# Attention's logits in a two-layer encoder trunk: the second product over 64 rows becomes one over 128

## The chip, the cores and the metric

The kernel runs on one core of one Trainium2 chip. The time is device microseconds of one execution; a profile records one execution and is a run of its own. The core has five engines with a queue of instructions each: TensorE (PE in the rows; its weight loads are shown apart as PEld), VectorE (DVE), ScalarE (ACT), GpSimd (POOL) and SyncE (SP). Each engine takes its own instructions in order and waits for the others by semaphores. Transfers between memory and the core's buffers are issued by SP, ACT or POOL.

## What is computed

Two layers over 512 frames of 1024 channels. In each layer a projection feeds a sparse attention with 8 heads of 64 channels, whose keys are chosen by an indexer, and a gated linear attention with 4 heads; both are merged, normalised, and followed by a gated convolution and feed-forward part. What matters here, from the reference:

```python
score = jnp.einsum('bqhs,bqh->bqs', jax.nn.relu(dots), wb.astype(F32) * (IDX_HEADS ** -0.5))
top_val, top_idx = lax.top_k(score, topk)
...
logits = jnp.einsum('bqhd,bqkhd->bhqk', qb.astype(F32), k_sel.astype(F32)) * (Dh ** -0.5)
logits = jnp.where(valid[:, None], logits, -jnp.inf)
p = jax.nn.softmax(logits, axis=-1)
return jnp.einsum('bhqk,bqkhd->bqhd', p, v_sel.astype(F32)).astype(q.dtype)
```

## The kernel before

Nearly all products work on float32 numbers split in two: a high part in the narrower format that TensorE takes, and the low part that is left (`split`, L145 on ScalarE for the high part and L146 on VectorE for the low one). A product of two split numbers is three products (`mm3`, L151 to L153). Weights come in tiles of 512 KB by SP, three raw tiles in flight and five split ones, and are split when a place is free.

The projections of queries and keys come out with one channel of each head per partition and are copied to device memory by GpSimd's queue, split (`staged`, L498), as a tile that holds the 64 high parts of a head in its first 64 rows and the 64 low parts in the others. `load_task` reads them back for two heads at a time: the keys as they are (L525), so that partitions 0 to 63 hold the high part of a head and 64 to 127 its low part, and the queries' high part into both halves of a tile (L529, two reads) with the low part in the first half of another (L530).

So a product of the queries' tile with the keys' tile over all 128 rows gives high times high plus high times low at once (L668), and a second one over 64 rows adds low times high (L669). `softmax_steps` does this for one head: four blocks of 128 queries, `qb` 0 to 3, against 128, 256, 384 and 512 keys. Both products go into one of two banks (`sps`), VectorE adds the mask and takes the maximum (L672), ScalarE takes the exponential (L675), VectorE divides (L676, L677). `values_steps` transposes (L697) and multiplies with the values (L706 to L709). The indexer's scores (L547 and L548) have two products over 128 rows each.

Attention is a task of generators that move on by two steps whenever the main work, a projection, has done a few products (`tick`). The order on each engine is settled when the program is built: the instructions are ordered by priorities and by modelled times, weight splits and the copies of projections out of their banks ahead of the rest. A change of the code can therefore move instructions that it doesn't touch.

Around the change the main work is, in this order: the queries' projection, the keys' (`ak`), the values' (`av`), and eight tiles of a gate (`gr_tile`), into which attention is woven. The four accumulation banks of `ak` are copied out and used again by `av`. At the same time the linear attention ends: VectorE takes the variance (L332), GpSimd its power -0.5 (L333), VectorE refines it (L336 to L339) and makes a shift (L646), ScalarE applies both (L652).

Of the kernel before, what the change touches and what calls it, by code (L numbers as in the profile page):

```python
# [10 lines left out]
F32 = mybir.dt.float32  # L11
# [45 lines left out]
class Trunk:  # L57
# [457 lines left out]
    def load_task(self, dr, dst, low=None):  # L515

        rows = dr.rearrange("(q h) n -> q h n", h=HEADS)
        load = self.nc.gpsimd.dma_start
        for _ in range(4):
            yield  # L520
        for hp in range(4):
            src = rows[:, 2 * hp:2 * hp + 2]
            t = self.u()
            if low is None:
                load(t.bitcast(F32), src)  # L525
            else:
                lo = self.u()
                for j in range(2):
                    load(t[64 * j:64 * j + 64].bitcast(F32), src[:64])  # L529
                load(lo[:64].bitcast(F32), src[64:])  # L530
                low.append(lo)
            yield
            yield
            dst.append(t)
        for _ in range(2):
            yield
# [120 lines left out]
    def softmax_steps(self, h, qT, kT, out):  # L657

        nc = self.nc
        hp = h // 2  # L660
        wide, slim = self.u(F32, (128, 1024)), self.h()
        at = {0: slim[:, 256:384], 1: slim[:, :256], 2: wide[:, 512:896], 3: wide[:, :512]}
        for qb in range(TB):
            n = 128 * (qb + 1)
            q = slice(qb * 128, (qb + 1) * 128)
            ps = self.bank(self.sps)
            k = kT[hp][:, h % 2, :n]
            nc.tensor.matmul(ps[:, :n], qT[hp][:, h % 2, q], k, start=True, stop=False)  # L668
            nc.tensor.matmul(ps[:, :n], self.ql[hp][:64, h % 2, q], k[:64], start=False, stop=True)  # L669
            lg = at[qb]  # L670
            mx = self.small([128, 4], tag="mx")
            nc.vector.tensor_tensor_reduce(out=lg, in0=ps[:, :n], in1=self.bias[qb], scale=1.0, scalar=TAKEN,  # L672
                                           op0=ALU.add, op1=ALU.max, accum_out=mx[:, 0:1])
            nc.vector.tensor_scalar(mx[:, 1:2], mx[:, 0:1], -(HD ** -0.5), None, op0=ALU.mult)
            nc.scalar.activation(lg, lg, AF.Exp, bias=mx[:, 1:2], scale=HD ** -0.5, accum_out=mx[:, 2:3])  # L675
            nc.vector.reciprocal(mx[:, 3:4], mx[:, 2:3])  # L676
            nc.vector.tensor_scalar(lg, lg, mx[:, 3:4], None, op0=ALU.mult)  # L677
            out.append(lg)
            yield
# [423 lines left out]
```

## Time and profile before

| | |
|---|---|
| time, median of 3 runs | 1791.14 us (1790.7 to 1793.73) |
| the profiled execution's own time | 1789.11 us |
| its span, first to last instruction | 1787.4 us |
| TensorE busy | 1766.6 us, 8312 products |
| TensorE weight loads busy | 1431.6 us |
| VectorE busy | 1130.4 us |
| ScalarE busy | 718.6 us |
| granted TensorE clock, mean | 0.998 of full speed |

Busy times count the work of an engine without its waits. Weight loads overlap with products, so the two TensorE rows can't be added. A product's row in the order of time lasts longer than the step from its start to the next start, since products follow each other through the array; the steps between starts are what a stretch is made of.

### The profile page before, as it was taken

What the parts mean: (1) busy time and instruction counts of PE and PEld (TensorE: products, weight loads), DVE (VectorE), ACT (ScalarE), POOL (GpSimd) and SP (SyncE); (2) the same over time, 40 slices, a digit from 0 to 9 for tenths busy, and PEclk for the clock granted to TensorE, in tenths of its full rate; (3) what the DMA queues carried; (4) which work ended last, traced back from release to release, by engine and by line L of the source; (5) the groups of instructions that cost most, each with busy time, mean ns of one, the idle gap of its engine ahead of it and who ended that gap; (6) DMA issues with size and microseconds to landing.
All of it is one profiled execution on the core that took longest, in us unless ns stands there. A gap on an engine that the chain in (4) does not pass through costs nothing.

```text
span 1787.4 us, 21711 instructions
## 1 busy us (share of the span) xinstructions
PE 1766.6 (99%) x8312; PEld 1431.6 (80%) x8312; DVE 1130.4 (63%) x2099; ACT 718.6 (40%) x1088; POOL 66.1 (4%) x105
## 2 busy tenths in 40 slices
PE   9999999999999999999999999999999999999997
PEld 7788777888888888888787878778888888888886
DVE  7699767733486663356667997776335766633656
ACT  6644456522225442144245454564232254422430
POOL 1000300000000000000010003000000000000000
PEclk9999999999999999999999999999999999999999
DMA  7322831233523322332353228212335233222331
GB/s 249 118 82 72 242 113 47 75 103 94 169 78 107 94 95 94 95 96 98 123 174 114 72 83 281 71 48 71 106 96 176 63 115 95 95 95 95 97 115 48
DMA packets 64531, 194.54 MB, mean 109 GB/s; under 512 B 7110, under 2 KB 9414, under 8 KB 64428
## 3 DMA queue, kind: packets, MB, share of 16 engines
q1 hardware_dynamic: 51312, 152.91, 27.2%
q0 software_dynamic: 7680, 27.27, 4.8%
q10 hardware_dynamic: 5436, 12.98, 2.1%
q8 instruction: 65, 1.06, 0.2%
q14 instruction: 38, 0.31, 0.1%
HBM read 176.36 MB, written 16.78 MB: 108 GB/s over the span
## 4 chain that ended last, share of the span: by engine, by line
PE 83%; DVE 12%; issue 2%; ACT 1%; POOL 1%; DMA 0%; DVEq 0%; SPq 0%; POOLq 0%; ACTq 0%
PE ps L151 26%; PE ps L152 26%; PE ps L153 26%; DVE w L146 2%; DVE sc L579 1%; PE ps L669 1%; DVE m L578 1%; PE ps L697 1%; DVE u L146 1%; DVE u L800 1%; DVE h L616 1%; PE ps L668 1%; POOL rs L333 1%; DVE xT L146 1%; PE ps L707 1%
## 5 line engine op out<-in xcount | busy, mean ns | idle before, releaser
L146 DVE TENSOR_TENSOR w<-raw,w 128x1024 fp32r<-128x1024 f32 (+2 forms) x287 | 349.7, 1218 | 486.6 <-ACT w L145 485.8
L151 PE MATMUL ps<-xT,w 128*128 128x512 f32 (+1 forms) x1456 | 555.4, 381 | 2.9 <-DVE xT L146 2.4
L153 PE MATMUL ps<-xT,w 128*128 128x512 f32 (+1 forms) x1456 | 551.5, 379 | 0.0
L152 PE MATMUL ps<-xT,w 128*128 128x512 f32 (+1 forms) x1456 | 551.2, 379 | 0.0
L145 ACT CAST w<-raw 128x1024 fp32r<-128x1024 f32 (+2 forms) x287 | 299.9, 1045 | 504.8 <-PE ps L153 446.2
L151 PEld LDWEIGHTS ps<-xT,w 128*128 128x128 f32 x1456 | 273.3, 188 | 61.4 <-ACT w L145 3.7
L153 PEld LDWEIGHTS ps<-xT,w 128*128 128x128 f32 x1456 | 273.4, 188 | 49.7
L152 PEld LDWEIGHTS ps<-xT,w 128*128 128x128 f32 x1456 | 273.4, 188 | 49.5 <-issue 0.5
L151 PE MATMUL ps<-w,u 128*128 128x512 f32 (+1 forms) x488 | 192.0, 393 | 0.0
L153 PE MATMUL ps<-w,u 128*128 128x512 f32 (+1 forms) x488 | 190.9, 391 | 0.0
L152 PE MATMUL ps<-w,u 128*128 128x512 f32 (+1 forms) x488 | 190.9, 391 | 0.0
L145 ACT CAST u<-h 128x512 fp32r<-128x512 f32 (+1 forms) x126 | 78.0, 619 | 219.7 <-DVE h L983 111.2
L146 DVE TENSOR_TENSOR u<-h,u 128x512 fp32r<-128x512 f32 (+1 forms) x126 | 86.2, 687 | 40.0 <-ACT u L145 39.6
L153 PEld LDWEIGHTS ps<-w,u 128*128 128x128 f32 x488 | 91.6, 188 | 21.6
L151 PEld LDWEIGHTS ps<-w,u 128*128 128x128 f32 x488 | 91.7, 188 | 21.3
L152 PEld LDWEIGHTS ps<-w,u 128*128 128x128 f32 x488 | 91.7, 188 | 20.7
L151 PE MATMUL ps<-w,xT 128*128 128x512 f32 x256 | 102.2, 399 | 0.2
L152 PE MATMUL ps<-w,xT 128*128 128x512 f32 x256 | 101.1, 395 | 0.0
L153 PE MATMUL ps<-w,xT 128*128 128x512 f32 x256 | 100.6, 395 | 0.0
L152 PE MATMUL ps<-u,w 128*128 128x512 f32 x192 | 76.0, 396 | 0.0
L151 PE MATMUL ps<-u,w 128*128 128x512 f32 x192 | 75.4, 393 | 0.0
L153 PE MATMUL ps<-u,w 128*128 128x512 f32 x192 | 74.6, 389 | 0.0
(221 smaller groups left out, 1905.4 us busy)
## 6 DMA issues: line engine op xcount, KB each, us to landing
raw<-in_w_fm SPq DMA_DIRECT2D x160, 512.0 KB, 3.6
raw<-in_w_tm SPq DMA_DIRECT2D x55, 512.0 KB, 3.6
raw<-in_w_down SPq DMA_DIRECT2D x44, 512.0 KB, 3.4
raw<-in_w_mix_out SPq DMA_DIRECT2D x16, 512.0 KB, 3.5
u<-aq POOLq DMA_DIRECT2D x24, 256.0 KB, 8.7
iq<-u POOLq DMA_DIRECT2D x8, 512.0 KB, 4.4
u<-iq POOLq DMA_DIRECT2D x8, 512.0 KB, 7.1
aq<-u POOLq DMA_DIRECT2D x8, 512.0 KB, 4.2
```

What stands on the lines that cost most here:

```text
L145: first = self.nc.scalar.copy(hi, src)
L146: self.nc.vector.tensor_sub(lo, src, hi.bitcast(F32))
L151: mm(out, lh, rl, start=start, stop=False)
L152: mm(out, ll, rh, start=False, stop=False)
L153: mm(out, lh, rh, start=False, stop=stop)
L333: self.nc.gpsimd.tensor_tensor(r, ve, self.nhalf[:, :n], ALU.pow)
L578: nc.vector.max(m8, sc)
L579: nc.vector.match_replace(sc, m8, sc, TAKEN)
L616: nc.vector.scalar_tensor_tensor(state[:, i], old[:, i], self.dec[:, h, c:c + 1], o[:, i], op0=ALU.mult, op1=ALU.add)
L668: nc.tensor.matmul(ps[:, :n], qT[hp][:, h % 2, q], k, start=True, stop=False)
L669: nc.tensor.matmul(ps[:, :n], self.ql[hp][:64, h % 2, q], k[:64], start=False, stop=True)
L697: nc.tensor.transpose(ps[:, qb * 128:(qb + 1) * 128], P[qb][:, sb * 128:(sb + 1) * 128], self.ident)
```

## The change

The queries' low part is read into both halves of its tile, one read more for each pair of heads (L530 moves into the loop), and the second product runs over all 128 rows, with the keys' whole tile. It now adds low times high and low times low.

```diff
                 lo = self.u()
                 for j in range(2):
                     load(t[64 * j:64 * j + 64].bitcast(F32), src[:64])
-                load(lo[:64].bitcast(F32), src[64:])
+                    load(lo[64 * j:64 * j + 64].bitcast(F32), src[64:])
                 low.append(lo)
...
             nc.tensor.matmul(ps[:, :n], qT[hp][:, h % 2, q], k, start=True, stop=False)
-            nc.tensor.matmul(ps[:, :n], self.ql[hp][:64, h % 2, q], k[:64], start=False, stop=True)
+            nc.tensor.matmul(ps[:, :n], self.ql[hp][:, h % 2, q], k, start=False, stop=True)
```

The order on the engines also changes, in the same way in both layers. On GpSimd, in the first layer, from the last read for heads 4 and 5 on (`aq` and `ak` are the copies of queries and keys in device memory, L498 writes them, `u` is a tile), before:

```order
L530 DMA u_1999<-aq_225 64x1024
L333 TENSOR_TENSOR rs_2010<-rs_2009,nhalf 128x8
L529 DMA u_2020<-aq_225 64x1024 x2
L530 DMA u_2021<-aq_225 64x1024
L498 DMA ak_226<-u_2062 128x2x512
L498 DMA ak_226<-u_2077 128x2x512
L498 DMA ak_226<-u_2088 128x2x512
L498 DMA ak_226<-u_2066 128x2x512
L525 DMA u_2140<-ak_226 128x1024
```

and after the change:

```order
L530 DMA u_2001<-aq_225 64x1024
L333 TENSOR_TENSOR rs_2013<-rs_2012,nhalf 128x8
L529 DMA u_2023<-aq_225 64x1024
L530 DMA u_2024<-aq_225 64x1024
L529 DMA u_2023<-aq_225 64x1024
L498 DMA ak_226<-u_2066 128x2x512
L498 DMA ak_226<-u_2081 128x2x512
L498 DMA ak_226<-u_2092 128x2x512
L498 DMA ak_226<-u_2070 128x2x512
L530 DMA u_2024<-aq_225 64x1024
L525 DMA u_2144<-ak_226 128x1024
```

Three more reads stand ahead of L333 (one for each earlier pair of heads), and the last read of the queries' low part now stands between the writes of the keys and their first read.

On VectorE, where the keys' banks are copied out (`ps_1830` and `ps_1831` are the first two of the four banks, `w` a weight tile), before:

```order
L506 TENSOR_TENSOR h_2050<-ps_1830,ropeT 64x512
L336 TENSOR_TENSOR rs_2011<-rs_2010 128x8
L507 TENSOR_TENSOR h_2049<-h_2049,h_2050 128x512
L337 TENSOR_TENSOR rs_2011<-rs_2011,rs_2009 128x8
L338 TENSOR_SCALAR rs_2011<-rs_2011 128x8
L339 TENSOR_TENSOR rs_2010<-rs_2010,rs_2011 128x8
L646 SCALAR_TENSOR_TENSOR sh_2035<-mv_1515,rs_2010 128x8
L146 TENSOR_TENSOR w_2131<-raw_2129,w_2131 128x1024
L146 TENSOR_TENSOR u_2062<-ps_1831,u_2062 128x512
```

and after:

```order
L506 TENSOR_TENSOR h_2054<-ps_1830,ropeT 64x512
L507 TENSOR_TENSOR h_2053<-h_2053,h_2054 128x512
L146 TENSOR_TENSOR w_2135<-raw_2133,w_2135 128x1024
L336 TENSOR_TENSOR rs_2014<-rs_2013 128x8
L337 TENSOR_TENSOR rs_2014<-rs_2014,rs_2012 128x8
L338 TENSOR_SCALAR rs_2014<-rs_2014 128x8
L339 TENSOR_TENSOR rs_2013<-rs_2013,rs_2014 128x8
L646 SCALAR_TENSOR_TENSOR sh_2039<-mv_1515,rs_2013 128x8
L146 TENSOR_TENSOR u_2066<-ps_1831,u_2066 128x512
```

The subtraction of a weight tile has moved ahead of the five small operations that end in the shift.

On ScalarE, at the same place, before:

```order
L145 CAST w_2131<-raw_2129 128x1024
L652 ACTIVATE u_1513<-u_1513,sh_2035,rs_2010 128x256
L145 CAST u_2062<-ps_1831 128x512
L145 CAST u_2066<-h_2049 128x512
L145 CAST u_2077<-ps_1832 128x512
L145 CAST u_2088<-ps_1833 128x512
L652 ACTIVATE u_1513<-u_1513,sh_2035,rs_2010 128x256 x3
```

and after:

```order
L145 CAST w_2135<-raw_2133 128x1024
L652 ACTIVATE u_1513<-u_1513,sh_2039,rs_2013 128x256 x2
L145 CAST u_2066<-ps_1831 128x512
L145 CAST u_2070<-h_2053 128x512
L145 CAST u_2081<-ps_1832 128x512
L145 CAST u_2092<-ps_1833 128x512
L652 ACTIVATE u_1513<-u_1513,sh_2039,rs_2013 128x256 x2
```

Two operations that need the shift, where one stood, come ahead of the cast of the keys' second bank. On TensorE one product (L153 of `av`'s first block) moves ahead of the first product into that bank; nothing else moves there or on SP.

## Rows read from the trace of the kernel before

**Rows 1.** The page: busy us by engine, and the chain that ended last.

```profile
PE 1766.6 (99%) x8312; PEld 1431.6 (80%) x8312; DVE 1130.4 (63%) x2099; ACT 718.6 (40%) x1088; POOL 66.1 (4%) x105
...
PE 83%; DVE 12%; issue 2%; ACT 1%; POOL 1%; DMA 0%; DVEq 0%; SPq 0%; POOLq 0%; ACTq 0%
```

**Rows 2.** Weight loads by line and shape: busy us, mean ns | idle before, releaser.

```profile
L669 PEld LDWEIGHTS ps<-u,u 64*128 64x128 f32 x64 | 11.7, 183 | 14.0 <-issue 12.4
...
L548 PEld LDWEIGHTS ps<-u,u 128*128 128x128 f32 x48 | 9.0, 188 | 2.1
```

**Rows 3.** Order of time, TensorE in attention: start us, us, engine, line, operation.

```profile
238.87 0.33 PE L668 MATMUL ps<-u,u 128*128 128x384 f32 x1
...
239.50 0.49 PE L668 MATMUL ps<-u,u 128*128 128x512 f32 x1
239.92 0.50 PE L669 MATMUL ps<-u,u 64*128 64x512 f32 x1
240.35 0.50 PE L151 MATMUL ps<-xT,w 128*128 128x512 f32 x1
240.69 0.39 PE L152 MATMUL ps<-xT,w 128*128 128x512 f32 x1
240.92 0.40 PE L153 MATMUL ps<-xT,w 128*128 128x512 f32 x1
```

**Rows 4.** Order of time, TensorE, attention's first products and the product behind them.

```profile
230.84 0.22 PE L668 MATMUL ps<-u,u 128*128 128x128 f32 x1
...
232.20 0.39 PE L152 MATMUL ps<-xT,w 128*128 128x512 f32 x1
```

**Rows 5.** Order of time, TensorE, index scores of 384 and of 256 columns.

```profile
84.36 0.33 PE L547 MATMUL ps<-u,u 128*128 128x384 f32 x1
84.36 0.19 PEld L548 LDWEIGHTS ps<-u,u 128*128 128x128 f32 x1
84.53 0.34 PE L548 MATMUL ps<-u,u 128*128 128x384 f32 x1
...
93.09 0.28 PE L547 MATMUL ps<-u,u 128*128 128x256 f32 x1
93.20 0.28 PE L548 MATMUL ps<-u,u 128*128 128x256 f32 x1
```

**Rows 6.** Stretch of attention, its length, busy us (count) of PE, PEld, DVE, ACT, POOL.

```profile
275.50:286.00 10.50, 10.47 (x47) 7.34 (x46) 8.73 (x29) 6.67 (x18) 0.00 (x0) 1.00 0.15 50
```

**Rows 7.** Order of time, all engines, where the keys' banks are copied out.

```profile
206.79 1.05 ACT L145 CAST w<-raw 128x1024 fp32r<-128x1024 f32 x1 [4.44 <-PE ps L153]
...
208.02 0.17 DVE L646 SCALAR_TENSOR_TENSOR sh<-mv,rs 128x8 f32<-128x8 f32 x1
...
208.10 1.22 DVE L146 TENSOR_TENSOR w<-raw,w 128x1024 fp32r<-128x1024 f32 x1
208.22 0.60 ACT L652 ACTIVATE u<-u,sh,rs 128x256 f32<-128x256 f32 x1 [0.37 <-DVE sh L646]
...
209.47 0.69 DVE L146 TENSOR_TENSOR u<-ps,u 128x512 fp32r<-128x512 f32 x1
...
210.21 0.19 PEld L151 LDWEIGHTS ps<-w,xT 128*128 128x128 f32 x1 [0.36 <-DVE u L146]
```

**Rows 8.** GpSimd's queue in order of time, then three groups of landings (202.54, 203.66, 222.79).

```profile
202.54 1.12 POOL L529 DMA_DIRECT2D u<-aq  x2
203.66 0.52 POOL L530 DMA_DIRECT2D u<-aq  x1
...
222.79 2.15 POOL L525 DMA_DIRECT2D u<-ak  x4 [8.84 <-DMA ak<-u]
...
DMA to landing us min/median/max: 9.2/9.8/10.5
...
DMA to landing us min/median/max: 11.7/11.7/11.7
...
DMA to landing us min/median/max: 5.3/5.3/5.3
```

## The prediction

> **What bounds the kernel now.** I read the page's totals first, then the chain that ended last, then the weight loads by group, then the order of time around the changed lines. TensorE is busy 1766.6 us of a span of 1787.4 us, and 83% of the chain runs over it [rows 1]. So a stretch that TensorE needs less time for shortens the kernel, as long as nothing it waits for comes later than it does now. VectorE is second with 12% of the chain and 63% of the span [rows 1].
>
> The changed product is L669. Its 64 weight loads stand behind 14.0 us of idle time on the weight-load side, 12.4 us of it put down to "issue", that is to no wait that the trace shows. The 48 loads of L548, the index scores' second product, have the same 128 columns of weights but all 128 rows, and 2.1 us [rows 2]. The order of time shows what that means. In the index scores, 384 columns, L548 starts 0.17 us after L547, and its weight load starts together with L547's product, so it is hidden; at 256 columns the step is 0.11 us [rows 5]. In attention the steps are longer: L668 with 512 columns to L669 0.42 us, L669 to L151 0.43 us, and L151 itself 0.34 us to the next product, where two products of full height follow each other in 0.23 us [rows 3]. The long steps are those between a product of 128 rows and one of 64, in both directions. I read this as: the load of weights of the other height does not start before the product ahead has gone through.
>
> **The change part by part.**
>
> *The second product over 128 rows.* The columns that stream through stay the same, so the product itself takes no longer; what goes are two changes of height for each of the 64 pairs. The pairs of 384 and 512 columns: from the first L668 to the second product of L151 and its kin, 238.87 to 240.69, 1.82 us [rows 3]. At the steps of full height it would be 2 x 0.17 + 3 x 0.23 = 1.03 us [rows 3, 5]. That is 0.79 us less. The pairs of 128 and 256 columns: 230.84 to 232.20, 1.36 us [rows 4], against 4 x 0.11 + 0.23 = 0.67 us, with the step of 256 columns taken for 128 columns too [rows 5]; 0.69 us less. A head is 1.48 us, and 8 heads in 2 layers make **23.7 us**. That is the upper end, since the rows of full height have no gap left; the lower end is 0, if the height is not the cause.
>
> The Trainium skill (TensorE: Matmul & The Clock Gate, Part 3: Packing small matmuls — row/col tiling) speaks against the gain: it says that a weight load overlaps products in flight only when its row group is another. Two products over all 128 rows share their row groups, so by that page the new load would be exposed too, and the gain would be near 0. The trace doesn't agree: the 128-row load of L548 starts in the same hundredth of a microsecond as L547's product, over the same rows [rows 5].
>
> *What VectorE gives back.* Each pair of products is followed by softmax work on VectorE, in the order of the program, and two banks hold the results. In 275.5 to 286 us VectorE is busy 8.73 of 10.5 us [rows 6]. About one head's saving, 1.48 us, falls into such a stretch, so it would last 9.0 us and VectorE would be 97% busy. It just fits, but not without waits. I take a tenth of the gain as lost, 2.4 us; the ends are 0 (the stretch stays longer than VectorE's work) and half (11.8 us).
>
> *The moved small work ahead of the keys' copies.* The added load puts GpSimd's reciprocal root (L333) later in its queue, and the order of VectorE and ScalarE changes with it, once in each layer. Now ScalarE has the weight cast until 206.79 + 1.05 = 207.84, one L652 at 208.22 to 208.82, then the cast of the keys' bank 1, whose subtraction starts on VectorE at 209.47 and ends at 210.16; TensorE's weight load for the next product into that bank starts at 210.21, after an idle 0.36 us that ends with this subtraction [rows 7]. After the change VectorE takes the weight subtraction first: 207.84 + 1.22 = 209.06. Then come five small operations, 0.17 us each and some 0.03 between, to 210.06; two L652, 2 x 0.60, to 211.26; the cast, 0.65 as now between 208.82 and 209.47; so the subtraction starts at 211.91, **2.4 us late**. TensorE has one product of 0.23 us more to fill the time, so it loses 2.2 us in each layer, 4.4 us in both. Nothing else can fill it: TensorE takes its products in order, and behind the waiting one stand the values' projection and all of attention. The ends: 0, if the later small operations overlap more than now, and 2.4 us a layer.
>
> *The eight added loads.* Four 256 KB reads a layer, on GpSimd's queue: three ahead of the keys' writes and the fourth between these and the keys' reads. Price of one: the loads issued at 202.54 and 203.66 land at 211.7 and 215.4, two loads apart, so 1.8 us each while the queue is full; the issue alone is 1.12 / 2 = 0.56 us [rows 8]. The first read of the keys is issued at 222.79, after waiting for the writes, and lands at 228.1; attention's first product runs at 230.84 [rows 4, 8]. The slack is 2.7 us, and 4.9 us with TensorE 2.2 us later. Four loads delay it by 2.2 us (at 0.56) to 7.2 us (at 1.8), so TensorE waits 0 to 2.4 us in a layer. I take 0.6 us for both together, since the fourth lies in the time in which the reads are on their way anyway.
>
> For one such load the Trainium skill (DMA: Bandwidth & Descriptors, Anatomy of one DMA — SWDGE (gpsimd) path) gives 2.0 us fixed plus the bytes at 436 GB/s, from which I estimate 0.6 us for what each adds to a full queue. By it the keys would not be late at all and the sum would be 0.6 us lower. The loads of 64 partitions in this trace are spaced three times as far [rows 8].
>
> *The sum.* -23.7 + 2.4 + 4.4 + 0.6 = -16.3 us. The profiled execution took 1789.11 us around its span of 1787.4, which gives 1772.8. The median of the runs shown, 1791.14, is 2.0 us above that execution, so I forecast **1774.8 us**.
>
> **The rivals.**
>
> *No late bank.* The keys' casts come no later than now and the reads are in time. For it: the 2.4 us rest on ScalarE waiting for the last of the small operations. Against: ScalarE takes its work in order, and L652 needs the result of L646 [rows 7]. The sum is -23.7 + 2.4, so 1769.8.
>
> *VectorE becomes the bound in attention.* For it: 97% of the shortened stretch. Against: a good part of VectorE's idle time there ends with the products that now come sooner. With half of the gain gone: -23.7 + 11.8 + 5.0 = -6.9, so 1784.2.
>
> *The gain isn't there, and the waits are.* The long steps come from something other than the height of the weights, and L669 at 128 rows keeps them. This ends slower: +5.0, so 1796. It decides once less than 5.0 of the 23.7 us come. Against it: the index scores have the same weights' width, the same columns and two banks, and no such step [rows 2, 5]. The Trainium skill's rule on row groups, above, would lead here.
>
> *The gain is used up.* Waits of 20 us or more would take an added load at three to four microseconds, twice the dearest row, or VectorE taking three quarters of the gain: no change.
>
> **How the numbers follow.** Forecast 0.62, no late bank 0.13, VectorE half 0.13, gain used up 0.05, slower 0.07. The range runs from the whole gain with no wait, 1791.1 - 23.7 = 1767, to VectorE's half, 1784; it leaves out little more than the last two. A measurement tells about 0.2%, 3.6 us, from no change. Faster by more than that: the first three, 0.88; no difference 0.05; slower 0.07.
>
> **What the new profile would show.** Right: L669's weight loads of 128 rows with little "issue" idle; L668 to L669 in 0.11 to 0.23 us by columns; the first product of L151 behind them without its 0.1 us; attention shorter by 10 to 12 us in each layer. The bank: TensorE idle some 2.2 us near 210 us and at the same place of the second layer. The loads: a short wait ahead of the first L668. Wrong: steps of 0.4 us between products of the same height, or TensorE waiting in attention for L672 or L677 on VectorE by more than 6 us a layer, or for the reads of the keys by more than 2.4 us.

## The result: 1.1% faster

The changed kernel takes 1773.09 us (median of 4, 1771.01 to 1777.13), the kernel before 1792.43 (median of 4): a ratio of 0.9892, with a 95% interval of 0.9875 to 0.9909, so 19.3 us less. The forecast was 1774.8 with a range of 1767 to 1784.2. The profiled execution took 1772.71 us, with a span of 1771.0, 16.4 less than the span before; why this is less than 19.3 is said below.

The page after: busy us by engine, and the chain by engine.

```profile
PE 1746.9 (99%) x8312; PEld 1429.8 (81%) x8312; DVE 1129.3 (64%) x2099; ACT 717.1 (40%) x1088; POOL 70.3 (4%) x113
...
PE 77%; DVE 14%; DMA 3%; issue 2%; ACT 2%; POOL 1%; SPq 0%; DVEq 0%; POOLq 0%; ACTq 0%
```

TensorE is busy 19.7 us less than in [rows 1], with as many products. Transfers now hold 3% of the chain, where they had nothing.

L669's weight loads after, in the columns of [rows 2]:

```profile
L669 PEld LDWEIGHTS ps<-u,u 128*128 128x128 f32 x64 | 12.1, 189 | 1.0
```

The 14.0 us of idle time ahead of L669's loads have become 1.0; nearly all that is gone was put down to "issue".

The order of time after, TensorE in head 1 (the pairs of 128 and 256 columns from 238.10 to 238.79, those of 384 and 512 from 239.95 to 240.99). [rows 3] has the same place before; [rows 4] has the pairs of 128 and 256 columns of head 0, 1.36 us, and head 1's took 1.37. (After, head 0's take 0.79, because its first product is the one that waits for the keys.)

```profile
238.10 0.22 PE L668 MATMUL ps<-u,u 128*128 128x128 f32 x1
...
238.79 0.40 PE L152 MATMUL ps<-xT,w 128*128 128x512 f32 x1
...
239.95 0.33 PE L668 MATMUL ps<-u,u 128*128 128x384 f32 x1
...
240.29 0.40 PE L668 MATMUL ps<-u,u 128*128 128x512 f32 x1
240.53 0.40 PE L669 MATMUL ps<-u,u 128*128 128x512 f32 x1
240.76 0.40 PE L151 MATMUL ps<-xT,w 128*128 128x512 f32 x1
240.99 0.40 PE L152 MATMUL ps<-xT,w 128*128 128x512 f32 x1
```

0.69 us where 1.37 stood, and 1.04 where 1.82 stood. L668 to L669 with 512 columns takes 0.24 us, L669 to L151 0.23, L151 to the next product 0.23: each step is that of two products of full height.

Attention as a whole, from its first product to the gate's first transpose (stretch, its length, busy us of PE, PEld, DVE, ACT, POOL, then the clock), first the kernel before, then after:

```profile
230.84:321.20 90.36, 90.23 (x418) 65.32 (x417) 65.58 (x216) 52.53 (x127) 0.00 (x0) 1.00 0.19 58
```

```profile
233.95:314.10 80.15, 79.87 (x417) 64.02 (x418) 64.75 (x215) 51.71 (x127) 0.00 (x0) 1.00 0.25 83
```

10.2 us less in the first layer, and as much in the second (from 90.36 to 80.17). VectorE does the same work, 65 us, and is now busy 81% of the stretch.

The keys' banks, to set beside [rows 7]:

```profile
209.71 0.50 PE L151 MATMUL ps<-w,xT 128*128 128x512 f32 x1
...
212.97 1.09 ACT L652 ACTIVATE u<-u,sh,rs 128x256 f32<-128x256 f32 x2 [2.19 <-DVE sh L646]
...
214.71 0.69 DVE L146 TENSOR_TENSOR u<-ps,u 128x512 fp32r<-128x512 f32 x1 [1.77 <-ACT u L145]
...
215.18 0.40 PE L153 MATMUL ps<-w,xT 128*128 128x512 f32 x1
...
215.45 0.19 PEld L151 LDWEIGHTS ps<-w,xT 128*128 128x128 f32 x1 [0.32 <-DVE u L146]
```

And the keys' reads (GpSimd's queue; landings of the four reads from 229.70 on), then TensorE at the first product of attention in each layer, with the product ahead of it:

```profile
229.70 2.15 POOL L525 DMA_DIRECT2D u<-ak  x4 [10.07 <-DMA ak<-u]
...
DMA to landing us min/median/max: 4.2/7.1/8.7
...
233.53 0.39 PE L153 MATMUL ps<-xT,w 128*128 128x512 f32 x1
...
233.95 0.33 PE L668 MATMUL ps<-u,u 128*128 128x128 f32 x1
...
1111.03 0.39 PE L153 MATMUL ps<-xT,w 128*128 128x512 f32 x1
...
1111.64 0.30 PE L668 MATMUL ps<-u,u 128*128 128x128 f32 x1 [0.23 <-DMA u<-ak]
```

The subtraction of bank 1 starts at 214.71 where it stood at 209.47, and TensorE's load behind it at 215.45 where it stood at 210.21. 2.95 us of these 5.24 were there before the queries were written (their first write is issued at 184.26, before at 181.31); the other 2.3 are the late bank. But TensorE doesn't stop for it: from 209.71 to 215.18 the trace has 24 products, 0.23 us from one to the next. The keys' first read lands at 229.70 + 4.2 = 233.9, and the first L668 starts at 233.95, 0.42 us after the product ahead of it, where 0.23 is the step between products: 0.2 us are lost. In the second layer it is 0.61 us, so 0.4 are lost.

### The profile page after: what moved, and what is told of

It is laid out like the page before. It is cut to its first block, busy times and chain, and to the rows that moved or that the text cites. A ratio compares the mean times of both kernels' runs of the same rounds, so it can differ in the third digit from the quotient of the medians.

```text
span 1771.0 us, 21726 instructions
## 1 busy us (share of the span) xinstructions
PE 1746.9 (99%) x8312; PEld 1429.8 (81%) x8312; DVE 1129.3 (64%) x2099; ACT 717.1 (40%) x1088; POOL 70.3 (4%) x113
## 2 busy tenths in 40 slices
DMA packets 65172, 196.65 MB, mean 111 GB/s; under 512 B 7238, under 2 KB 9542, under 8 KB 65068
## 3 DMA queue, kind: packets, MB, share of 16 engines
q0 software_dynamic: 8320, 29.36, 5.3%
## 4 chain that ended last, share of the span: by engine, by line
PE 77%; DVE 14%; DMA 3%; issue 2%; ACT 2%; POOL 1%; SPq 0%; DVEq 0%; POOLq 0%; ACTq 0%
PE ps L152 24%; PE ps L151 24%; PE ps L153 24%; DVE w L146 2%; DVE sc L579 2%; DVE m L578 1%; DVE u L146 1%; PE ps L697 1%; DVE u L800 1%; DVE h L616 1%; DMA u<-aq 1%; POOL rs L333 1%; DMA raw<-in_w_tm 1%; PE ps L707 1%; DVE xT L146 1%
## 5 line engine op out<-in xcount | busy, mean ns | idle before, releaser
L151 PE MATMUL ps<-xT,w 128*128 128x512 f32 (+1 forms) x1456 | 553.7, 380 | 3.0 <-DVE xT L146 2.5
L153 PE MATMUL ps<-xT,w 128*128 128x512 f32 (+1 forms) x1456 | 551.2, 379 | 0.0
L151 PEld LDWEIGHTS ps<-xT,w 128*128 128x128 f32 x1456 | 273.7, 188 | 56.0 <-ACT w L145 3.3
L153 PEld LDWEIGHTS ps<-xT,w 128*128 128x128 f32 x1456 | 273.5, 188 | 50.7
L151 PE MATMUL ps<-w,u 128*128 128x512 f32 (+1 forms) x488 | 192.0, 393 | 0.0
L153 PE MATMUL ps<-w,u 128*128 128x512 f32 (+1 forms) x488 | 190.9, 391 | 0.0
L153 PEld LDWEIGHTS ps<-w,u 128*128 128x128 f32 x488 | 91.6, 188 | 21.6
L151 PEld LDWEIGHTS ps<-w,u 128*128 128x128 f32 x488 | 91.7, 188 | 21.4
L151 PE MATMUL ps<-w,xT 128*128 128x512 f32 x256 | 102.2, 399 | 0.2
L153 PE MATMUL ps<-w,xT 128*128 128x512 f32 x256 | 100.9, 395 | 0.0
L151 PE MATMUL ps<-u,w 128*128 128x512 f32 x192 | 75.4, 393 | 0.0
L153 PE MATMUL ps<-u,w 128*128 128x512 f32 x192 | 74.6, 388 | 0.0
## 6 DMA issues: line engine op xcount, KB each, us to landing
u<-aq POOLq DMA_DIRECT2D x32, 256.0 KB, 11.1
```

The source lines that it names most:

```text
L151: mm(out, lh, rl, start=start, stop=False)
L153: mm(out, lh, rh, start=False, stop=stop)
```

## The experiments

One theory stood against three rivals. **Height:** weights of 64 rows among weights of 128 cost at each change from one to the other, and nothing else in attention matters. **The rivals:** a load of 64 rows can't be hidden whatever stands ahead of it; or the new order and the loads brought the gain; or the cost belongs to attention's two banks.

**The cost of the change without its gain.** The loads stay, and the product is taken back:

```diff
-            nc.tensor.matmul(ps[:, :n], self.ql[hp][:, h % 2, q], k, start=False, stop=True)
+            nc.tensor.matmul(ps[:, :n], self.ql[hp][:64, h % 2, q], k[:64], start=False, stop=True)
```

> The changed kernel's loads and its order on every engine, but the second product over 64 rows as before; so it has the cost of the change without the gain. Height theory (the time lies in the changes between weights of 128 and of 64 rows): attention as long as before, 90.4 us from its first product to the gate's first transpose, and in all 0 to 1 us above the kernel before, since TensorE filled the wait for the keys' bank with ten more products of the values' first block. The prediction's own step on the late bank: +4.4 and +0.6, so 5.0 us slower (ratio 1.003). Rival, that the new order or the loads brought the gain: 16 to 20 us faster (0.99).

Measured: ratio 1.0005 (0.9996 to 1.0014), which is -0.7 to +2.5 us. Attention, and L669's loads:

```profile
234.86:325.22 90.36, 90.23 (x419) 65.37 (x418) 65.56 (x216) 52.57 (x127) 0.00 (x0) 1.00 0.21 71
...
L669 PEld LDWEIGHTS ps<-u,u 64*128 64x128 f32 x64 | 11.7, 183 | 13.8 <-issue 12.1
```

Attention takes 90.36 us, to the hundredth what it took before, with the same 12 us of "issue". So the loads and the order bring none of the gain. They cost at most 2.5 us, half of the 5.0 that the prediction set down for them.

**96 rows.** The same again with `self.ql[hp][:96, h % 2, q]` and `k[:96]`.

> The changed kernel with the second product over 96 rows of the same tiles: low times high, and low times the first half of low; the other half of low times low is left out. Any change of height costs: 128 to 96 and back costs as 128 to 64 did, the time of the kernel before (ratio 1.00). Only heights that belong to another division of the array cost, and 96 rows need the whole of it: the time of the changed kernel (0.989).

Measured: 0.9893 (0.988 to 0.9907). Attention, and L669's loads:

```profile
232.05:312.20 80.15, 79.93 (x417) 64.16 (x418) 64.58 (x215) 51.55 (x126) 0.00 (x0) 1.00 0.24 82
...
L669 PEld LDWEIGHTS ps<-u,u 96*128 96x128 f32 x64 | 12.1, 189 | 1.1
```

80.15 us and 1.1 us of idle time: 96 rows behave as 128. So it is not any change of height that costs, and a product doesn't have to fill the array. 64 rows cost and 96 don't.

**The same 64-row products in another order.** The kernel before, with two blocks' products taken together:

```diff
+            for b in (qb, qb + 1) if qb % 2 == 0 else ():
+                banks[b] = self.bank(self.sps)
+            for low in range(2) if qb % 2 == 0 else ():
+                for b in (qb, qb + 1):
...
-            nc.tensor.matmul(ps[:, :n], qT[hp][:, h % 2, q], k, start=True, stop=False)
-            nc.tensor.matmul(ps[:, :n], self.ql[hp][:64, h % 2, q], k[:64], start=False, stop=True)
```

> The kernel before, with the two blocks of queries that move on together taken as high, high, low, low instead of high, low, high, low; 64 rows stay. The changes of height fall from 4 to 2 for two blocks, the 64-row loads stay as many. Height theory: half of the 20.4 us of attention, 10 us less (ratio 0.994), and the second L669 starts 0.11 to 0.23 us after the first. Rival, that a load of 64 rows can't be hidden behind anything: 3 exposed loads instead of 4, 5 us less (0.997), and the second L669 starts 0.3 to 0.4 us after the first.

Measured: 0.9972 (0.9961 to 0.9982), 5 us, which is the rival's number. The order of time in head 0 (the first product of 128 rows is L675 here, the one of 64 rows L673; x2 stands for both blocks), then attention as a whole:

```profile
232.31 0.39 PE L675 MATMUL ps<-u,u 128*128 128x128 f32 x2
...
233.39 0.39 PE L152 MATMUL ps<-xT,w 128*128 128x512 f32 x1
...
234.54 0.57 PE L675 MATMUL ps<-u,u 128*128 128x384 f32 x2
235.03 0.68 PE L673 MATMUL ps<-u,u 64*128 64x384 f32 x2
235.64 0.50 PE L151 MATMUL ps<-xT,w 128*128 128x512 f32 x1
235.98 0.39 PE L152 MATMUL ps<-xT,w 128*128 128x512 f32 x1
```

```profile
232.31:320.37 88.06, 88.00 (x420) 64.97 (x419) 64.96 (x216) 53.74 (x128) 0.00 (x0) 1.00 0.17 55
```

The total is the rival's, but the rows speak against it. 128 and 256 columns take 232.31 to 233.39, 1.08 us: 0.28 less than before and 0.39 more than after; 384 and 512 columns take 1.44, 0.38 less and 0.40 more. That is half of the gain. The two 64-row products of 384 and 512 columns, with the second one's weight load:

```profile
235.14 0.19 PEld L673 LDWEIGHTS ps<-u,u 64*128 64x128 f32 x1
...
235.32 0.39 PE L673 MATMUL ps<-u,u 64*128 64x512 f32 x1
```

The second product starts 0.29 us after the first, more than the 0.11 to 0.23 of the height theory and just under the 0.3 of the rival; by this number alone neither is right. But the second load starts at 235.14, while the first product runs, and ends when the second product starts, so it is hidden behind a product of its own height. The step is about 0.11 us above the 0.17 of full height because the first product itself started late, after a change: L151, the product behind the next change, also takes 0.34 us to the next one, 0.11 above 0.23, and there both are of 128 rows.

The total is small because the order was kept only in places. In the trace, changes between 128 and 64 rows in attention fall from 128 to 100, not to 64: only 14 of the 64 products of L673 stand directly behind another. Attention lost 90.36 - 88.06 = 2.3 us in this layer and 2.2 in the other. 4.5 us by 28 changes is 0.16 us a change; the whole change took away 128, for 20.4 us, which is 0.16 too. By the rival one exposed load would have been saved in each of these 14 places, 2.2 us at the same price. My expectation had counted the code and not the order of the built program.

**The cost put elsewhere.** The changed kernel, with the index scores' second product over 64 rows:

```diff
-        mm(out, q, kl, start=False, stop=True)
+        mm(out, q[:64], kl[:64], start=False, stop=True)
```

> The changed kernel, with the index scores' second product (the queries' tile times the keys' low part) over 64 rows instead of 128; what is left out is the queries' low part times the keys' low part. Height theory: 48 pairs get two changes of height each, at the 0.32 us a pair that attention gave back, 15 us more than the changed kernel, about 1788 (0.998 of the kernel before), with steps of 0.32 to 0.43 us where 0.11 to 0.23 stood. Rival, that the long steps belong to attention (its two banks and what VectorE does with them): no more than 1 us above the changed kernel (0.989).

Measured: 1.0002 (0.9992 to 1.0012) of the kernel before; it gives the whole gain back. The order of time at a pair of 384 columns (L547, L548, and the two products behind them), then L548's loads:

```profile
83.82 0.33 PE L547 MATMUL ps<-u,u 128*128 128x384 f32 x1
84.08 0.44 PE L548 MATMUL ps<-u,u 64*128 64x384 f32 x1
84.45 0.50 PE L151 MATMUL ps<-w,xT 128*128 128x512 f32 x1
84.79 0.39 PE L152 MATMUL ps<-w,xT 128*128 128x512 f32 x1
```

```profile
L548 PEld LDWEIGHTS ps<-u,u 64*128 64x128 f32 x48 | 8.8, 183 | 14.3 <-issue 14.3
```

0.97 us, where steps of full height make 2 x 0.17 + 0.23 = 0.57. The "issue" idle is now at L548, 14.3 us, and L669's line is the one shown above for the changed kernel, with 1.0. Nothing of attention is needed for the cost. It is larger than expected: every pair here stands alone among projection products and pays 0.40 us, and 48 of them make 19 us.

**The changed kernel again.**

> The changed kernel once more, beside the next two on the same chip: 19 us less than the kernel before (ratio 0.988 to 0.991). In its trace the start, up to the queries' projection, tells whether the 3 us by which it came later in the first profile belong to the change (then again about 3 us) or to that execution (then anything from 0 to 3).

Measured: 0.9887 (0.9872 to 0.9901). Attention in both layers, and two of TensorE's waits:

```profile
231.78:311.99 80.21, 79.99 (x419) 63.92 (x418) 64.88 (x216) 51.88 (x127) 0.00 (x0) 1.00 0.25 82
1109.80:1189.95 80.15, 79.90 (x417) 64.03 (x418) 64.49 (x215) 51.56 (x126) 0.00 (x0) 1.00 0.23 81
...
PE ps L668 <- DMA u<-ak: 0.5, 1, 0.5
PE ps L469 <- ACT h L401: 0.4, 1, 0.4
```

The second of these waits in the kernel before, and in the first profile after:

```profile
PE ps L469 <- ACT h L401: 1.1, 1, 1.1
...
PE ps L469 <- ACT h L401: 3.1, 1, 3.1
```

80.2 us in both layers again. The wait of L469 for ScalarE's L401, at about 38 us, long before attention, is 0.4 us here and was 3.1 in the first profile after, of the same program; before it was 1.1. Behind the 3.1 us the granted clock stood at 0.51 from 40 to 42 us and at 0.63 from 42 to 44, and at 1.00 in the other two profiles. So 2.0 of the 2.95 us by which the first profile started late are this wait, and the lower clock adds to it; they belong to that execution, and its span hides 3 us of the gain. The first write of the queries, at 181.31 before and 184.26 after, is issued at 182.29 here, at 182.00 with 96 rows and at 185.36 with the loads only. Spans of single profiles differ by this start; the changed kernel's attention doesn't (80.15 to 80.21 us).

**One transfer for both halves.** An attempt at a better version:

```diff
-                    load(t[64 * j:64 * j + 64].bitcast(F32), src[:64])
-                    load(lo[64 * j:64 * j + 64].bitcast(F32), src[64:])
+                load(t.bitcast(F32), src[:64].unsqueeze(0).to_broadcast(both))
+                load(lo.bitcast(F32), src[64:].unsqueeze(0).to_broadcast(both))
```

> The changed kernel with the queries' high and low part each read into both halves by one transfer of 128 partitions and 512 KB instead of two of 64 partitions and 256 KB: 8 reads a layer instead of 16 for the same bytes. If the queue is held by the number of 64-partition reads, the reads of the queries end some 8 us sooner, the reads of the keys are issued as early as before the change or earlier, TensorE no longer waits 0.2 us for them, and the time is 0 to 1 us below the changed kernel (0.2% can't be told). If bytes hold the queue, nothing moves. If reading one source twice in a transfer is slow, attention's first product waits, several us more.

Measured: 0.9998 (0.9983 to 1.0012): it loses all of the gain. GpSimd's queue, its reads of the queries (median us to landing), and the wait:

```profile
q0 software_dynamic: 22400, 29.42, 5.6%
...
u<-aq POOLq DMA_DIRECT2D x16, 512.0 KB, 26.6
...
PE ps L668 <- DMA u<-ak: 16.3, 2, 8.3
```

The reads take 26.6 us to land, where the changed kernel's took 11.1, and the queue sends 22400 packets instead of 8320. The 14080 more are all under 512 B (21318 such packets in this page, 7238 in the changed kernel's), and the bytes grow only from 29.36 to 29.42 MB: the data goes in as many large packets as before, with small ones added. The keys' writes and reads queue behind them, and TensorE waits 16.3 us. The order of time around the first wait, and the clock (the column ahead of the last two):

```profile
246.41 0.47 PE L668 MATMUL ps<-u,u 128*128 128x128 f32 x1 [8.35 <-DMA u<-ak]
...
247.44 0.63 PE L151 MATMUL ps<-xT,w 128*128 128x512 f32 x1
247.86 0.63 PE L152 MATMUL ps<-xT,w 128*128 128x512 f32 x1
...
245.00:250.00 5.00, 3.59 (x11) 3.01 (x11) 0.92 (x6) 0.99 (x4) 0.00 (x0) 0.50 0.94 348
260.00:280.00 20.00, 20.00 (x105) 15.95 (x104) 14.37 (x50) 11.40 (x27) 0.00 (x0) 1.00 0.20 65
```

After the 8.35 us of waiting, products follow each other in 0.42 us instead of 0.23: the granted clock is 0.50 from 245 to 250 us, the lower of its two levels (1.2 GHz), and 1.00 again from 260. Why a transfer that reads its source twice adds so many small packets, and whether they make it slow, stays open.

**No second product.** To see whether VectorE would have become the bound:

```diff
-            nc.tensor.matmul(ps[:, :n], qT[hp][:, h % 2, q], k, start=True, stop=False)
-            nc.tensor.matmul(ps[:, :n], self.ql[hp][:, h % 2, q], k, start=False, stop=True)
+            nc.tensor.matmul(ps[:, :n], qT[hp][:, h % 2, q], k, start=True, stop=True)
```

> The changed kernel without the second product at all: the queries' low part is read and never used, so low times high and low times low are left out. It takes another 5.1 us of TensorE's time from attention in each layer. If VectorE has slack there, attention falls to 75 us and the time by 10 us below the changed kernel (0.983 to 0.984 of the kernel before). The prediction's rival, VectorE as the bound of the shortened stretch: attention stays near 80 us and the time within 2 us of the changed kernel.

Measured: 0.985 (0.9827 to 0.9873), 1765.3 us, 6 below the changed kernel on the same chip; its four runs spread from 1760.0 to 1770.7. Attention in both layers, and a wait:

```profile
235.97:311.70 75.73, 75.29 (x386) 59.44 (x387) 63.23 (x215) 52.28 (x128) 0.00 (x0) 1.00 0.25 87
1110.61:1187.92 77.31, 76.88 (x387) 60.61 (x388) 62.19 (x214) 52.14 (x127) 0.00 (x0) 0.98 0.24 80
...
PE ps L668 <- DMA u<-ak: 1.9, 1, 1.9
```

Attention falls by 4.4 us in the first layer and by 2.9 in the second. There 1.9 us of waiting for the keys stand just ahead of it, and behind this wait the granted clock is 0.50 from 1112 to 1114 us, which goes with the stretch's 0.98. The time fell by 6 us and not by the 10 that were expected without a bound; attention accounts for 7.3. TensorE now waits 0.7 us for VectorE ahead of L668, which the changed kernel's waits don't have. So VectorE's work of 63 us nearly follows when TensorE needs 5 us less. The rival, which had attention stay near 80 us, is refuted at the length that the change gives; the run doesn't tell where VectorE would bind.

## Why the prediction was right, step by step

- **The gain of the second product:** right in kind, somewhat too large. 23.7 us were worked out from the pairs of head 0 and 1, which gave 1.48 us; they came as forecast there (0.68 and 0.78). Over all heads the two layers gave 20.4 us, 1.28 a head. Part of the rest is seen: the steps from start to start of L668 and L669, added up over the first layer's attention, come to 10.7 us after, where 8 heads at the steps of full height would take 8 x (4 x 0.11 + 2 x 0.17 + 2 x 0.23) = 9.9. The term was extrapolated from two heads whose pairs stand among projection products alone; the later ones are woven into transposes and the values' products. In the traces the pairs of 256 to 512 columns with a transpose behind them gave back 0.32 to 0.35 us, those with a projection product behind them 0.39 to 0.47. The rest was not followed further.
- **VectorE's tenth, 2.4 us:** not found as idle time of TensorE, which is 0.3 us in attention after. On the weight-load side the waits for VectorE grew from 2.1 to 3.1 us in the first layer's attention, partly hidden behind products. So up to 1 us a layer of what is missing from 23.7 can be VectorE's; how much of it is was not separated from the term above.
- **The late bank, 4.4 us:** the step failed. The bank is late by 2.3 us, as worked out, but TensorE loses nothing there. I had compared TensorE's order before and after with the banks' numbers left out, and found one product moved, as the section on the change says. With the numbers, 24 products of the values' first block stand ahead of the second bank, where 14 stood; the ten more fill 10 x 0.23 = 2.3 us. The lateness was sized well; the sentence that nothing else can fill the time was wrong.
- **The loads, 0.6 us:** right in size, 0.2 + 0.4 us in the two layers of the first profile after, and 0.6 in the second layer alone of the other (0.5 of it shown as a wait). In part this is luck: the 0.6 was taken with a TensorE that comes 2.2 us later, and it doesn't. The keys' read is issued 229.70 - 222.79 - 2.95 = 4.0 us late. The late bank has a part in that, since it delays the keys' writes by 2.3 us; so a load costs between 0.4 us (the rest by four) and 1.0, less than the 1.8 of the full queue.
- **The sum:** -16.3 forecast, -19.3 measured and -20.4 in attention. The bank and the loads were 5.0 us of it; the run that has them alone allows 2.5 at most, and its trace shows no wait of TensorE for the keys. Attention's 20.4 less the 0.6 of waits make 19.8, beside the 19.3 measured. That the forecast lies so near is partly luck: the gain less VectorE's tenth, 21.3, was 0.9 us too high, and the bank's 4.4 didn't come. And the forecast started from a median of 1791.14, where the kernel before now has 1792.43; so the times differ by 1.7 us, and the gains by 3.0.

The rival "no late bank" gives 1769.8. Its condition, casts that come no later, was not met, but what it has TensorE lose there, nothing, is what the runs showed; the median of the second measurement, 1771.38, lies between it and the forecast.

The Trainium skill's rule that a weight load overlaps only products of another row group (TensorE: Matmul & The Clock Gate, Part 3: Packing small matmuls — row/col tiling) doesn't hold for these runs: L669's loads over all rows have 1.0 us of idle time ahead of them, against 14.0 for those over half the rows [rows 2]. The Trainium skill says elsewhere (TensorEngine Tiling (Array Packing), Tiling Modes, Key Properties) that a change of tiling mode drains TensorE. The runs agree for rows: 128 to 64 and back costs 0.16 us a change, a load of 64 rows behind 64 is hidden (at 235.14 above), and 96, which the page doesn't list as a mode, goes as 128 (80.15 us of attention). That TensorE drains at a change is the page's reason; the runs show the cost and where it falls.

## What to carry to other kernels

A product over 64 rows among products over 128 can cost more than one over 128: count the changes in the built order, price them by the step from start to start (0.16 us a change in attention, 0.2 where a pair stands alone), and fill the tile, if the other half has something harmless or useful to add. A late buffer costs only what TensorE can't do meanwhile, and this is read from the built order with its buffer numbers.

## What was not expected of the hardware

Weights of 96 rows are loaded and followed as those of 128 (80.15 us of attention in both). A read of 64 rows into 128 partitions in one transfer took 26.6 us to land where two transfers of half the size took 11.1 each. Behind a wait of 8.35 us the granted clock stood at 0.50 for the next products, and so it did behind shorter ones: 3.1 us in the first profile after (0.51 from 40 to 42 us), 1.9 us without the second product (0.50 from 1112 to 1114). A wait can so cost more than its own length.
